# Moving one branch's weight sums out of the marked queue, and one order of four sums

## The chip, the cores and the metric

The kernel runs on one core of one Trainium2 chip. The metric is the device time of one execution in microseconds, as the median of several runs. Engines are named TensorE (PE in the rows; PEld is its weight load), VectorE (DVE), ScalarE (ACT), GpSimd (POOL) and SyncE (SP).

## What is computed

One layer of a streaming encoder on 512 positions of width 1024, all in float32:

```python
h = rmsnorm(x, norm_mix)
u, v, bg, cg, xb, zc, gl = split(h @ w_in)
ya = sgu(gelu(u), gelu(v), ...)          # gated, masked 128x128 blocks
yb = bg * causal_dwconv(cg * xb, conv_b_w)
yc = pool_mixer(zc, pool_w, pool_scale)
g  = sigmoid(gl)                         # three gates, 1024 wide each
merged = g[0] * (ya @ w_br_a) + g[1] * (yb @ w_br_b) + g[2] * (yc @ w_br_c)
x = x + merged @ w_o
h = rmsnorm(x, norm_ffn)
a = causal_dwconv(h @ w_up, ffn_conv_w)
x = x + (silu(a_gate) * a_value) @ w_down
out = rmsnorm(x, norm_f)
```

The change lies around the three branch products (`ya @ w_br_a` and so on) and the three gates' columns of `h @ w_in`.

## The kernel before

**Products in three parts.** A float32 matrix is split into an upper part (ScalarE copies it to the rounded type, `upper`, or negated in `split_negative`, L59 and L63) and a lower part (VectorE subtracts, `lower`, L67 and L64). `mm3` (L81 to L83) issues upper times upper and both mixed products, so each product costs three matmuls of 128 x 512.

**Seven instead of eight.** The branches, the gates and the down projection are 2 x 2 block products done with seven block products (m1 to m7) instead of eight. They need four sums of weight blocks, T1 to T4. For the first two branches VectorE adds the blocks in SBUF (`add_branch`, L166, its adds are L178). For the third branch, the gates and the down projection the sums are made in HBM: a `WeightSums` object (L135) has four HBM tensors; `copy` copies a base block into each and `add` issues accumulating transfers on top. T1 = b11 + b12, T2 = b22 + T1, T3 = b12 + b22, T4 = b21 + T2. So T2's add needs T1, and T4's needs T2. For a gate each block is 1 MB, for a branch 0.5 MB. All these transfers are issued by POOL's queue q0, in the written order (`in_order`, L127). An add waits on POOL until its base copy, and the sum it reads, have landed; what stands behind it on POOL waits too.

**Feeding TensorE.** SP loads blocks of 128 x 1024 weights into raw tiles (`Raws`, L92, queue q1); four may be live, and the next is issued when VectorE has finished with one. `Pieces` (L332) gives the order: branch 0, gate 0, branch 1, gate 1, branch 2, gate 2, one piece for a branch's block product, two for a gate's. Each piece is split into one of four ring slots, which is free again when TensorE has used the piece four before it. A piece is 12 matmuls. The order inside ScalarE's and VectorE's queues is laid out before the run by a planner, which goes by its own estimates of durations; only in the head of the kernel the written order is kept.

**Around the change.** At L634 to L637 POOL, after a tiny wait, issues copies and adds of gate 0's and gate 1's sums. The sums of branch 2 and gate 2 come later, behind marks: the list `behind` (L927 to L930) holds eleven steps (one of four copies, four adds of branch 2; two of two copies, four adds of gate 2), and `next_sum` (L932) takes one off: ScalarE copies a column of the bank o just written to a tiny tile (L936), POOL copies that tile (L407), and so waits until TensorE has come so far; then POOL issues the step. `gate` (L959) calls `next_sum` after each of its seven products, `branch` (L1028) after form s2 for branches 1 and 2. Seven steps therefore fall in gate 0, one in branch 1, three in gate 1.

In `branch` the bank x takes m1, is copied by ScalarE (`copies`, L948, tile bm), and then takes form s2 on top; later x takes s3, VectorE adds it into c (L842), and then a22. So TensorE's s2 waits for bm, and a22 waits for VectorE's c. The tile bm shares its scratch buffers with the gate's last s (L961), which VectorE reads at the end of the gate.

Of the kernel before, what the change touches and what calls it, by code (L numbers as in the profile page):

```python
# [26 lines left out]
def trunk_kernel(  # L27
# [64 lines left out]
    class Raws:  # L92


        def __init__(self):
            self.todo, self.ready, self.live, self.cap = [], [], 0, 4
# [38 lines left out]
    class WeightSums:  # L135
        def __init__(self, name, b11, b12, b21, b22):
            t1, t2, t3, t4 = self.t = [
                dram.tile([P, b11.shape[1], 528], F32, name=f"{name}_t{i + 1}")[:, :, :512] for i in range(4)]
            self.base = [(t1, b11), (t3, b12), (t2, b22), (t4, b21)]
            self.added = [(t1, b12), (t3, b22), (t2, t1), (t4, t2)]  # L140

            self.products = {"m1": b11, "m2": b21, "m3": b22, "m4": t4, "m5": t1, "m6": t2, "m7": t3}

# [96 lines left out]
    def tiny(tag, name):  # L240
        return small.tile([P, 1], F32, tag=tag, name=name)
# [156 lines left out]
    def quarters(half, c0):  # L398
        return [half(k)[:, :, c0 + 512 * h:c0 + 512 * h + 512] for k in range(2) for h in range(2)]

    gate_sums = [WeightSums(f"g{i}", *quarters(lambda k: w_in_v[:, 4 * k:4 * k + 4], 3072 + 1024 * i))
                 for i in range(3)]
    last_branch_sums = WeightSums("br2", *quarters(lambda k: w_br_q[2][k], 0))

    def pool_waits_for(t, name):

        in_order(nc.gpsimd.tensor_copy(tiny(name, name), t[:, 0:1]))  # L407
# [224 lines left out]
        v_gelu(t)  # L632
    v_center()
    pool_waits_for(pw_raw, "begun")  # L634
    for sums in gate_sums[:2]:
        sums.copy()
        sums.add()  # L637

# [181 lines left out]
    def form(tags, name):  # L820

        return [[act.tile([P, 2, 256], F32R, tag=tags[2 * kp + i], name=f"{name}_{p}{kp}")
                 for i, p in enumerate(("hi", "lo"))] for kp in range(2)]
# [17 lines left out]
    def tt(o, a, b, op):  # L841
        nc.vector.tensor_tensor(o, a, b, op=op)  # L842
# [41 lines left out]
    sums = []  # L884
# [39 lines left out]
    nc.vector.tensor_scalar(nrstd1, rstd1, -1.0, None, op0=ALU.mult)  # L924


    behind = [lambda: last_branch_sums.copy()]  # L927
    behind += [lambda: last_branch_sums.add(1)] * 4
    behind += [lambda: gate_sums[2].copy(2)] * 2
    behind += [lambda: gate_sums[2].add(1)] * 4  # L930

    def next_sum(o):  # L932
        if behind:
            n = len(behind)
            mark = tiny(f"mark{n}", f"mark{n}")
            nc.scalar.copy(mark, o[:, 0:1])  # L936
            pool_waits_for(mark, f"passed{n}")
            behind.pop(0)()

    def product(o, st, n, first):  # L940
        for q in range(0, n, 2):
            [w] = pieces.take()
            for k in range(q, q + 2):
                mv = [p[:, 512 * (k - q):512 * (k - q) + 512] for p in w]
                for r in range(2):
                    mm3(o[r], st(k, r), mv, first and k == 0, k == n - 1, more=not first)

    def copies(tag, name, o):  # L948
        got = [scratch(tag, f"{name}{r}") for r in range(2)]
        for r in range(2):  # L950
            nc.scalar.copy(got[r], o[r])
        return got

    def banks(name):
        return [bank(f"{name}{r}") for r in range(2)]
# [72 lines left out]
    def branch(i, form):  # L1028
        c = [[act.tile([P, S], F32, tag=f"m{8 + 2 * t + h}" if i == 0 else f"x{t}{h}", name=f"c{i}{t}{h}")
              for h in range(2)] for t in range(NT)]  # L1030
        x = banks(f"bx{i}")
        product(x, form("a11"), 2, True)
        m1 = copies(0, f"bm1{i}", x)
        d = banks(f"bd{i}")
        product(d, form("s1"), 2, True)
        m5 = copies(1, f"bm5{i}", d)
        product(x, form("s2"), 2, False)
        if i > 0:
            next_sum(x[1])
        m16 = copies(2, f"bm16{i}", x)  # L1040
        a = banks(f"ba{i}")
        product(a, form("a12"), 2, True)
        for r in range(2):
            tt(c[r][0], a[r], m1[r], ALU.subtract)
        product(x, form("s3"), 2, False)
        for r in range(2):
            tt(c[2 + r][1], x[r], m5[r], ALU.add)
        product(d, form("s4"), 2, False)
        for r in range(2):
            tt(c[r][1], d[r], m16[r], ALU.add)  # L1050
        product(x, form("a22"), 2, False)
        for r in range(2):
            nc.scalar.mul(c[2 + r][0], x[r], -1.0)
        return c

    for i in range(3):
        c = branch(i, forms[i])
        if i == 0:
            acc = c
        gate(i, c)  # L1060
# [221 lines left out]
    x = banks("dx")  # L1282
# [83 lines left out]
```

## Time and profile before

| what | value |
|---|---|
| median of 3 runs | 739.06 us (738.57 to 740.81) |
| profiled execution | 736.67 us |
| its span, first to last instruction | 734.9 us |
| TensorE busy | 720.7 us, 98% of the span |
| VectorE, ScalarE, POOL busy | 562.7, 370.6, 62.6 us (77%, 50%, 9%) |
| DMA moved | 150.87 MB, mean 205 GB/s |
| POOL's queue q0, SP's queue q1 | 52.43 MB, 96.76 MB |
| chain that ended last | PE 93%, DVE 3%, DMA 2%, ACT 1% |

The profile is one execution, taken on the core, and its durations belong to that execution alone. The busy time of TensorE is modelled at the ends of matmuls, so the steps between starts say more than the busy share. An idle time in brackets behind a row is that of the engine just before the instruction, with what ended it; a wait for several things is put down to the last of them that the profile can see.

### The profile page before, as it was taken

The numbers are of one execution on the slowest core, as the hardware profiler recorded it, in microseconds if no ns is written. First come the engines' busy times: TensorE is split into PE (matmuls) and PEld (weight loads), VectorE is DVE, ScalarE is ACT, GpSimd is POOL, SyncE is SP. The second block draws the span as 40 slices with busy tenths as digits, with TensorE's granted clock in tenths as the row PEclk, the third lists the DMA queues.
The fourth block names the chain that finished last, engine by engine and source line by source line (L and its number), as shares of the span: only waits on it lengthen the run. The fifth ranks groups of instructions, "written<-read, shape, count | busy, mean of one in ns | idle before, by whom it ended". The sixth has DMA issues, their size and how long they took to land.

```text
span 734.9 us, 8928 instructions
## 1 busy us (share of the span) xinstructions
PE 720.7 (98%) x3258; PEld 594.8 (81%) x3258; DVE 562.7 (77%) x836; ACT 370.6 (50%) x551; POOL 62.6 (9%) x93
## 2 busy tenths in 40 slices
PE   8999999999999998999999999999999999999996
PEld 5888888888877886888888888888888888888885
DVE  6889899889598687677556786766787776997674
ACT  4744144266675565664444443443444444965453
POOL 0041210001221100000012010100000000000110
PEclk9999999999999999999999999999999999999999
DMA  8649999737999996675228999999633232576652
GB/s 254 192 170 283 244 331 237 183 90 232 304 313 313 229 295 199 196 225 183 87 75 264 236 296 285 253 311 220 178 97 105 86 106 82 155 234 201 194 163 114
DMA packets 89211, 150.87 MB, mean 205 GB/s; under 512 B 4008, under 2 KB 39248, under 8 KB 89168
## 3 DMA queue, kind: packets, MB, share of 16 engines
q1 hardware_dynamic: 68607, 96.76, 41.7%
q0 software_dynamic: 19840, 52.43, 29.8%
q10 hardware_dynamic: 720, 1.11, 0.4%
q8 instruction: 25, 0.41, 0.2%
q14 instruction: 19, 0.15, 0.1%
HBM read 148.20 MB, written 54.53 MB: 276 GB/s over the span
## 4 chain that ended last, share of the span: by engine, by line
PE 93%; DVE 3%; DMA 2%; ACT 1%; issue 1%; SPq 0%; ACTq 0%
PE pug L83 5%; PE puv L83 5%; PE pug L81 5%; PE puv L81 5%; PE puv L82 5%; PE pug L82 5%; PE gx L82 3%; PE gx L81 3%; PE gx L83 3%; PE dx L83 2%; PE dx L82 2%; PE po L81 2%; PE dx L81 2%; PE po L83 2%; PE po L82 2%; PE gd L83 1%
## 5 line engine op out<-in xcount | busy, mean ns | idle before, releaser
L81 PE MATMUL pug<-h2T_hi,ring_hi 128*128 128x512 f32 x176 | 68.7, 390 | 0.0
L83 PE MATMUL pug<-h2T_hi,ring_lo 128*128 128x512 f32 x176 | 68.5, 389 | 0.0
L82 PE MATMUL puv<-h2T_lo,ring_hi 128*128 128x512 f32 x176 | 68.5, 389 | 0.0
L81 PE MATMUL puv<-h2T_hi,ring_hi 128*128 128x512 f32 x176 | 68.5, 389 | 0.0
L82 PE MATMUL pug<-h2T_lo,ring_hi 128*128 128x512 f32 x176 | 68.5, 389 | 0.0
L83 PE MATMUL puv<-h2T_hi,ring_lo 128*128 128x512 f32 x176 | 68.5, 389 | 0.0
L67 DVE TENSOR_TENSOR ring_lo<-raw_g_m,ring_hi 128x1024 fp32r<-128x1024 f32 x30 | 36.6, 1224 | 29.2 <-ACT ring_hi L59 29.1
L59 ACT CAST ring_hi<-raw_ug 128x1024 fp32r<-128x1024 f32 x22 | 23.3, 1057 | 47.4 <-PE pug L82 42.2
L67 DVE TENSOR_TENSOR ring_lo<-raw_uv,ring_hi 128x1024 fp32r<-128x1024 f32 x22 | 26.9, 1222 | 25.1 <-ACT ring_hi L59 25.1
L59 ACT CAST ring_hi<-raw_g_m 128x1024 fp32r<-128x1024 f32 x30 | 31.5, 1055 | 26.2 <-DMA raw_g_m<-in_w_in_dram 9.6
L67 DVE TENSOR_TENSOR ring_lo<-raw_d_m,ring_hi 128x1024 fp32r<-128x1024 f32 (+1 forms) x30 | 35.8, 1204 | 9.0 <-ACT ring_hi L59 8.9
L59 ACT CAST ring_hi<-raw_d_m 128x1024 fp32r<-128x1024 f32 (+1 forms) x30 | 29.5, 982 | 18.6 <-PE da L83 8.2
L82 PEld LDWEIGHTS puv<-h2T_lo,ring_hi 128*128 128x128 f32 x176 | 33.0, 188 | 6.9
L82 PEld LDWEIGHTS pug<-h2T_lo,ring_hi 128*128 128x128 f32 x176 | 33.0, 188 | 6.9
L83 PEld LDWEIGHTS pug<-h2T_hi,ring_lo 128*128 128x128 f32 x176 | 33.0, 188 | 6.9
L83 PEld LDWEIGHTS puv<-h2T_hi,ring_lo 128*128 128x128 f32 x176 | 33.0, 188 | 6.9
L81 PEld LDWEIGHTS puv<-h2T_hi,ring_hi 128*128 128x128 f32 x176 | 33.0, 188 | 6.9
L81 PEld LDWEIGHTS pug<-h2T_hi,ring_hi 128*128 128x128 f32 x176 | 33.0, 188 | 6.8
L67 DVE TENSOR_TENSOR ring_lo<-raw_ug,ring_hi 128x1024 fp32r<-128x1024 f32 x22 | 26.9, 1222 | 8.8 <-ACT ring_hi L59 8.7
L59 ACT CAST ring_hi<-raw_uv 128x1024 fp32r<-128x1024 f32 x22 | 23.2, 1056 | 19.1 <-PE puv L82 18.8
L1136 ACT ACTIVATE av<-av_y,colv 128x512 f32<-128x512 f32 x22 | 16.0, 727 | 27.9 <-DVE av_y L1134 26.9
L1136 ACT ACTIVATE ag<-ag_y,colv 128x512 f32<-128x512 f32 x22 | 15.8, 720 | 21.5 <-DVE ag_y L1134 21.5
(432 smaller groups left out, 2028.9 us busy)
## 6 DMA issues: line engine op xcount, KB each, us to landing
g_t<-in_w_in_dram POOLq DMA_DIRECT2D x18, 1024.0 KB, 13.2
d_t<-in_w_down_dram POOLq DMA_DIRECT2D x6, 2816.0 KB, 27.2
raw_g_m<-g_t SPq DMA_DIRECT2D x24, 512.0 KB, 4.2
raw_ug<-in_w_up_dram SPq DMA_DIRECT2D x22, 512.0 KB, 6.2
raw_uv<-in_w_up_dram SPq DMA_DIRECT2D x22, 512.0 KB, 5.1
raw_d_m<-d_t SPq DMA_DIRECT2D x20, 512.0 KB, 3.9
raw_g_m<-in_w_in_dram SPq DMA_DIRECT2D x18, 512.0 KB, 10.0
raw_d_m<-in_w_down_dram SPq DMA_DIRECT2D x15, 512.0 KB, 3.3
```

Of the source, the lines that this page charges most:

```text
L59: return keep(nc.scalar.copy(hi, src))
L67: return keep(nc.vector.tensor_tensor(lo, src, hi.bitcast(F32), op=ALU.subtract))
L81: keep(nc.tensor.matmul(o, st[0], mv[0], start=first, stop=False, **skip))
L82: keep(nc.tensor.matmul(o, st[0], mv[1], start=False, stop=False, **skip))
L83: keep(nc.tensor.matmul(o, st[1], mv[0], start=False, stop=last, **skip))
L1136: nc.scalar.activation(a, y, AF.Copy, scale=ffn_w(2, c))
```

## The change

Three edits. The order of base copies and adds in every `WeightSums` is T1, T2, T3, T4 instead of T1, T3, T2, T4 (it holds for all gates, branch 2 and the down projection). Branch 2's four copies and four adds are issued right behind gate 1's, without marks. Of the list behind marks eight steps remain, gate 2's copies and adds one by one; `branch` no longer takes a step. So gate 0's seven products take seven steps and gate 1's first product the eighth.

```diff
         def __init__(self, name, b11, b12, b21, b22):
             t1, t2, t3, t4 = self.t = [
                 dram.tile([P, b11.shape[1], 528], F32, name=f"{name}_t{i + 1}")[:, :, :512] for i in range(4)]
-            self.base = [(t1, b11), (t3, b12), (t2, b22), (t4, b21)]
-            self.added = [(t1, b12), (t3, b22), (t2, t1), (t4, t2)]
+            self.base = [(t1, b11), (t2, b22), (t3, b12), (t4, b21)]
+            self.added = [(t1, b12), (t2, t1), (t3, b22), (t4, t2)]
...
     pool_waits_for(pw_raw, "begun")
-    for sums in gate_sums[:2]:
+    for sums in gate_sums[:2] + [last_branch_sums]:
         sums.copy()
         sums.add()
...
-    behind = [lambda: last_branch_sums.copy()]
-    behind += [lambda: last_branch_sums.add(1)] * 4
-    behind += [lambda: gate_sums[2].copy(2)] * 2
+    behind = [lambda: gate_sums[2].copy(1)] * 4
     behind += [lambda: gate_sums[2].add(1)] * 4
...
         product(x, form("s2"), 2, False)
-        if i > 0:
-            next_sum(x[1])
         m16 = copies(2, f"bm16{i}", x)
```

## Rows read from the trace of the kernel before

**Rows 1.** TensorE's timeline: start us, duration, line, tiles, [idle before <-releaser]

```profile
216.93 0.50 PE L81 MATMUL bx<-ring_hi,f_hi 128*128 128x512 f32 x1 [0.54 <-ACT bm L951]
...
227.03 0.39 PE L83 MATMUL bd<-ring_hi,f_lo 128*128 128x512 f32 x1
...
229.14 0.47 PE L81 MATMUL bx<-ring_hi,fo_hi 128*128 128x512 f32 x1 [1.72 <-DVE c L842]
...
275.27 0.39 PE L83 MATMUL bd<-ring_hi,f_lo 128*128 128x512 f32 x1
...
278.37 0.65 PE L81 MATMUL bx<-ring_hi,f_hi 128*128 128x512 f32 x1 [2.71 <-ACT bm L951]
...
282.35 0.40 PE L82 MATMUL bx<-ring_lo,f_hi 128*128 128x512 f32 x1
```

**Rows 2.** Window: span, busy of PE, PEld, DVE, ACT, POOL; PEclk; DMA share; GB/s

```profile
278.40:281.80 3.40, 3.40 (x8) 2.64 (x9) 3.10 (x3) 2.44 (x4) 0.00 (x0) 0.52 0.59 166
```

**Rows 3.** Timeline of ScalarE, columns as in the first group

```profile
163.74 1.06 ACT L63 ACTIVATE ring_hi<-raw_g_m 128x1024 fp32r<-128x1024 f32 x1 [1.17 <-PE ba L83]
...
226.07 1.06 ACT L63 ACTIVATE ring_hi<-raw_g_m 128x1024 fp32r<-128x1024 f32 x1 [3.62 <-DMA raw_g_m<-in_w_in_dram]
...
270.04 1.05 ACT L59 CAST ring_hi<-raw_br_m 128x1024 fp32r<-128x1024 f32 x1 [4.37 <-PE gx L82]
...
277.74 1.19 ACT L951 COPY bm<-bx 128x512 f32<-128x512 f32 x2 [1.41 <-DVE c L842]
```

**Rows 4.** Timeline of VectorE

```profile
228.31 1.28 DVE L842 TENSOR_TENSOR c<-bx,bm 128x512 f32<-128x512 f32 x2
...
271.13 1.23 DVE L67 TENSOR_TENSOR ring_lo<-raw_br_m,ring_hi 128x1024 fp32r<-128x1024 f32 x1 [1.31 <-ACT ring_hi L59]
```

**Rows 5.** Timeline of POOL: the sums' transfers

```profile
132.77 1.02 POOL L151 DMA_DIRECT2D g_t<-g_t  x1 [12.56 <-issue]
...
177.89 2.81 POOL L146 DMA_DIRECT2D br_t<-in_w_br_c_dram  x4
...
206.83 1.55 POOL L146 DMA_DIRECT2D g_t<-in_w_in_dram  x2
...
259.36 1.02 POOL L151 DMA_DIRECT2D g_t<-g_t  x1 [10.31 <-issue]
```

**Rows 6.** Timeline of SP: the loads, merged

```profile
155.77 8.45 SPq L106 DMA_DIRECT2D raw_g_m<-in_w_in_dram  x4
...
218.53 5.57 SPq L106 DMA_DIRECT2D raw_g_m<-in_w_in_dram  x4
...
261.47 1.84 SPq L106 DMA_DIRECT2D raw_br_m<-br_t  x2
```

**Rows 7.** Three more windows, columns as in the second group

```profile
100.00:204.50 104.50, 104.50 (x463) 86.53 (x462) 88.09 (x126) 52.15 (x74) 12.54 (x16) 1.00 0.82 225
...
145.00:155.00 10.00, 10.00 (x46) 8.29 (x45) 9.15 (x12) 3.77 (x6) 0.00 (x0) 1.00 0.00 0
...
211.00:221.00 10.00, 9.46 (x41) 7.16 (x40) 10.00 (x12) 8.91 (x18) 1.77 (x3) 1.00 1.01 362
```

**Rows 8.** Tile view of one load each, issued at 163.9, 245.5 and 265.1

```profile
DMA to landing us min/median/max: 3.5/3.5/3.5
...
DMA to landing us min/median/max: 13.6/13.6/13.6
...
DMA to landing us min/median/max: 7.4/7.4/7.4
```

**Rows 9.** DMA queues: packets, MB, share; 211 to 221, then 247 to 256

```profile
q0 software_dynamic: 932, 3.60, 100.8%
...
q0 software_dynamic: 592, 1.18, 70.5%
...
q1 hardware_dynamic: 594, 1.15, 38.8%
```

**Rows 10.** Page, DMA issues: count, KB each, median us to landing

```profile
g_t<-in_w_in_dram POOLq DMA_DIRECT2D x18, 1024.0 KB, 13.2
```

## The prediction

> **What bounds the kernel now.** TensorE does, nearly everywhere. So I read first the timeline of TensorE's matmuls and looked only for places where the step from one start to the next is longer than usual: what TensorE doesn't lose, no other engine can give back. In [rows 1] the usual step follows from the starts at 216.93 and 227.03 us, 44 steps apart: 10.10 / 44 = 0.23 us. Between 20 us and the tail I find three places with more than 0.2 us to lose, all in the second and third branch:
>
> - A1, at 216.93: TensorE idle 0.54 us ahead of bx (branch 1, form s2), released by ScalarE's copy bm. Loss 0.5 us.
> - A2, at 229.14: 2.11 us after the last matmul of bd, less a step of 0.23: loss 1.9 us. Released by VectorE (L842, c).
> - B, at 278.37: from 275.27 to 282.35 us lie 11 steps, 7.08 - 11 * 0.23 = 4.6 us lost. The wait itself (on ScalarE's bm in branch 2) is 2.71 us; the rest is the granted clock, 0.52 in the 3.4 us behind the gap [rows 2], the lower of its two levels, after TensorE had stood still.
>
> Together 7.0 us, 0.95% of the run. That is all there is to win; the head, the tail and the dense rest aren't touched by the edit.
>
> Next I asked who was late at each of them, in the timelines of ScalarE and VectorE. At A2, ScalarE stood 3.62 us until 226.07 for the first weights of gate 1 [rows 3]; VectorE's lower half of that split came behind it, and only then c<-bx,bm at 228.31, which frees the bank that TensorE wants [rows 4]. So one late transfer in VectorE's fixed order holds TensorE. SP issued it at 218.53 [rows 6]: 7.5 us to landing, where a like transfer with nothing beside it took 3.5 [rows 8]. In those microseconds POOL's copies for gate 2 (two issued from 206.83, two behind the next mark) [rows 5] were running: from 211 to 221 us POOL's queue q0 had the DMA engines whole, 3.60 MB in 10 us [rows 9].
>
> At B, ScalarE stood 4.37 us and began a raw_br_m at 270.04 [rows 3]. The row names a matmul, but the raw was issued at 261.47 [rows 6], and SP's next but one, issued at 265.10, took 7.4 us [rows 8], to 272.5; I read 270.0 as the landing, 8.5 us after the issue. Beside it ran the last add of gate 2, issued at 259.36 [rows 5]. VectorE waited 1.31 us for that split at 271.13 [rows 4], and from there its timeline shows no idle time up to the c that ScalarE's bm waited for until 277.74 [rows 3]. So A2 and B start as transfers that met POOL's sums. A1 doesn't: VectorE is busy 10.00 of the 10 us around it [rows 7], with four extra adds (L178) per branch.
>
> **The change, part by part.**
>
> *Branch 2's sums without marks.* Four copies and four adds of 0.5 MB leave their five places among the marks and stand behind gate 1's last add, issued at 132.77 [rows 5]. POOL, SP's loads and the DMA engines are what they pass: from 145 to 155 us the DMA share is 0.00 [rows 7], and the first loads of gate 0 come at 155.77 [rows 6]. With marks its issues took from 177.89 until gate 2's copies at 206.83, 29 us, and a landing more. Eight issues with three dependent landings I estimate at 25 to 40 us, so they end between 160 and 175 us. ScalarE's split of gate 0's first weights starts only at 163.74, when TensorE frees a slot [rows 3]; the load issued at 155.77 may take 8.0 us instead of 3.5 before that moves. I book 0; bounds 0 and +5 us (latency of 13.6 as in [rows 8]: 5.6 us late, in the pattern of A2).
>
> *Three marks gone* (11 become 8; branch 1 has none any more): each a tiny ScalarE copy, a tiny POOL copy and waits, all beside matmuls. 0 us on the path; bounds -0.2 and 0 at A1, where one stood in ScalarE's queue.
>
> *Gate 2's sums from the first mark on.* The marks come every (206.83 - 177.89) / 5 = 5.8 us [rows 5]. So four copies of 1 MB go at about 178, 183, 189 and 195 us, one each, where before 2 MB of branch 2's copies went at once and 2 MB of its adds followed. The first add goes at 201; a landing takes POOL some 13 us [rows 10], so the second and third are held in POOL's queue and issued at 212 to 215; the fourth at gate 1's first mark, near 237. What is queued behind POOL's wait is only the next mark's copy and sums: nobody on the path before gate 2 reads T2. Over gate 0 some 5 MB move instead of 4 plus the 4 MB burst at its end. Booked 0 for gate 0: from 100 to 204.5 us, gate 1's sums and then branch 2's beside it, TensorE was busy all 104.50 us [rows 7]. Bounds 0 and +3 us (one block of loads late: 12 matmuls of 0.23 us).
>
> *A2.* Its load at 218.53 now meets two adds instead of the end of a burst of copies. An add shares: from 247 to 256 us q0 moved 1.18 MB and SP's q1 1.15 MB [rows 9], so 0.52 MB take 9 * 0.52 / 1.15 = 4.1 us. Ahead of it lie the 3.5 us of an undisturbed load less its 0.52 MB at 362 GB/s [rows 7], 1.4 us: 2.1. So I estimate the landing at 218.5 + 6.2 = 224.7, 1.3 us sooner. Loss left 1.9 - 1.3 = 0.6 us; bounds 0 (adds late) and 2.9 (B's load, first in its queue beside a fresh add, took 8.5 us: landing 227.0). I take the share, since here the adds have been running for some us when the load comes.
>
> The Trainium skill (DMA: Bandwidth & Descriptors, section Queues, rings and completion order) states that each DMA engine goes round-robin between the queue rows that it has work for, a packet at a time. The adds agree (1.18 to 1.15 MB [rows 9]); the copies from 218.5 to 221 don't, q0 kept everything. By the rule alone A2 would already have had its half and would not improve: 1.3 us less gain.
>
> *B.* No sum runs after about 250 us; the load takes 3.5 instead of 8.5 us, and the split is bound by its ring slot, about 265, not 270. VectorE then gets 5 us for five splits and adds that it now does in a row; the wait was 2.71. Loss left 0 us; bounds 0 and 3.3 (VectorE's own 1.31 us of idle is all that comes back).
>
> *T2 ahead of T3* in copies and adds: T2's add waits for T1's landing, so T3's stands behind it on POOL; T4's wait then overlaps T3's transfer. Each gate has one empty latency either way. 0 us; what it serves, gate 2's T2 first, isn't waited for.
>
> Sum: A1 stays 0.5, A2 leaves 0.6, B 0: 7.0 - 1.1 = 5.9 us less. The profiled execution took 736.67 us with a span of 734.9; the three timed runs have the median 739.06 (738.57 to 740.81). I take the difference off the median: 733.2 us. 0.3% (2.2 us) is about what a measurement of this kernel can tell from no change.
>
> **The rivals.**
>
> *VectorE, not the load, sets B.* Its queue is gapless from 271.13 to B's end, which speaks for it; against it, 4 us of ScalarE's idle ahead say the work could have been done earlier. Then only 1.3 us come back at B and the low clock stays, and nothing sure at A2: 739.06 - 1.3 = 737.8, no change that can be told.
>
> *Gate 1's first loads still late.* The adds held on POOL come out at 212 to 215, straight onto the load of 218.53. Against: adds share, the copies didn't [rows 9]. A2 stays at 1.9: 739.06 - 4.6 = 734.5.
>
> *Slower: the chain of branch 2's sums ends too late.* Place: POOL, 133 to 178 us [rows 5]. If its last add lands after the first mark (177.9), gate 2's sums all slip and reach B again, so the 7.0 us stay, while gate 0's loads from 155.77 on meet adds that they didn't meet. With a landing later than 163.7 VectorE stands in branch 0 as it did at A2, and TensorE loses about what B lost: 739.06 + 4.6 = 743.7. It decides at a chain of 45 us instead of my 25 to 40. The planner that lays out each engine's order beforehand may place a split badly with the same result; nothing in the trace tells.
>
> **How the numbers follow.** Forecast (731.5 to 735.5) 0.47; late loads in gate 1 (734.5) 0.20; VectorE at B (737.8) 0.17; slower (743.7) 0.16. Faster by over 0.3%, below 736.8: 0.47 + 0.20 + 0.03 of the VectorE case = 0.70. Within: 0.14. Slower: 0.16. The range runs from 731.2 (all 7.0 us gone and 0.9 of spread between runs) to 741.2, which leaves out most of the slower case; the likeliest case's own range is 731.5 to 735.5.
>
> **What would show it.** Right: the DMA share from 145 to 155 us far from 0; br_t's last add issued before 170; no add issued after 250; bx of branch 2 follows bd within 0.5 us at full clock; the wait at bx of branch 1 (form a22) below 1 us. Wrong in part: bx still waits on bm although its load landed 3.5 us after the issue (VectorE). Wrong altogether: TensorE's first gap in branch 0 or gate 0, between 150 and 210 us, or a gap after 284.

## The result, and the profile after

The changed kernel takes 731.12 us (median of 4, 730.71 to 733.10) against 738.82 (median of 4, 737.35 to 740.81) for the kernel before: ratio 0.9899, 95% interval 0.9870 to 0.9929, so 5.2 to 9.6 us less. The profiled executions have spans of 734.9 and 729.3 us.

TensorE's list of waits after the change (us in total, times, longest) has one entry left behind the head of the kernel:

```profile
PE bx L81 <- DVE c L842: 1.6, 1, 1.6
```

The gaps of [rows 1], in TensorE's timeline after the change:

```profile
215.36 0.39 PE L83 MATMUL bd<-ring_hi,f_lo 128*128 128x512 f32 x1
215.59 0.39 PE L81 MATMUL bx<-ring_hi,f_hi 128*128 128x512 f32 x1
...
274.35 0.39 PE L83 MATMUL bd<-ring_hi,f_lo 128*128 128x512 f32 x1
274.57 0.39 PE L81 MATMUL bx<-ring_hi,f_hi 128*128 128x512 f32 x1
```

A1 and B are gone: form s2 follows bd one step (0.23 us) later in branch 1 (215.59) and in branch 2 (274.57). A2 is still there: a wait of 1.6 us on the same c. The sums, in POOL's timeline after:

```profile
125.03 1.02 POOL L151 DMA_DIRECT2D g_t<-g_t  x1 [6.70 <-issue]
125.66 3.21 POOL L146 DMA_DIRECT2D br_t<-in_w_br_c_dram  x4
...
155.54 0.89 POOL L151 DMA_DIRECT2D br_t<-br_t  x1 [4.36 <-issue]
178.26 0.77 POOL L146 DMA_DIRECT2D g_t<-in_w_in_dram  x1
...
199.93 1.19 POOL L151 DMA_DIRECT2D g_t<-in_w_in_dram  x1
211.44 1.06 POOL L151 DMA_DIRECT2D g_t<-g_t  x1 [5.11 <-DMA g_t<-in_w_in_dram]
213.29 1.15 POOL L151 DMA_DIRECT2D g_t<-in_w_in_dram  x1
239.17 1.02 POOL L151 DMA_DIRECT2D g_t<-g_t  x1
```

Branch 2's sums stand between 125.66 and 155.54, gate 2's last add at 239.17 instead of 259.36 [rows 5]. Windows after (span, busy of PE, PEld, DVE, ACT, POOL, granted clock, DMA share, GB/s), for the three of [rows 7]:

```profile
100.00:204.50 104.50, 104.50 (x463) 86.60 (x462) 87.32 (x124) 53.34 (x75) 15.22 (x21) 1.00 0.94 265
145.00:155.00 10.00, 10.00 (x46) 8.29 (x45) 9.15 (x13) 3.66 (x5) 1.98 (x2) 1.00 0.74 119
211.00:221.00 10.00, 10.00 (x45) 8.28 (x45) 9.62 (x13) 9.40 (x16) 3.00 (x3) 1.00 0.84 145
```

The stretch from 145 to 155 us, empty before, now carries 0.74 of the DMA engines' time, and TensorE stays busy throughout. Nor were gate 0's first loads hurt: ScalarE still waits there for TensorE's slot, as at 163.74 in [rows 3].

```profile
164.11 1.06 ACT L63 ACTIVATE ring_hi<-raw_g_m 128x1024 fp32r<-128x1024 f32 x1 [1.17 <-PE ba L83]
```

### The profile page after: what moved, and what is told of

Same layout as the page of the kernel before. It is cut to its first block, busy times and chain, and to the rows that moved or that the text cites. A ratio compares the mean times of both kernels' runs of the same rounds, so it can differ in the third digit from the quotient of the medians.

```text
span 729.3 us, 8922 instructions
## 1 busy us (share of the span) xinstructions
PE 718.5 (99%) x3258; PEld 594.4 (82%) x3258; DVE 562.7 (77%) x836; ACT 370.2 (51%) x548; POOL 60.2 (8%) x90
## 4 chain that ended last, share of the span: by engine, by line
PE 94%; DMA 3%; ACT 1%; DVE 1%; issue 0%; SPq 0%; ACTq 0%
PE pug L83 5%; PE puv L83 5%; PE pug L81 5%; PE puv L82 5%; PE pug L82 5%; PE puv L81 5%; PE gx L83 3%; PE gx L81 3%; PE gx L82 3%; PE dx L82 2%; PE dx L83 2%; PE po L81 2%; PE dx L81 2%; PE po L83 2%; PE po L82 2%; PE dd L82 1%
## 5 line engine op out<-in xcount | busy, mean ns | idle before, releaser
L1132 ACT ACTIVATE av<-av_y,colv 128x512 f32<-128x512 f32 x22 | 15.9, 724 | 27.9 <-DVE av_y L1130 26.9
```

What stands on the lines that cost most here:

```text
L1132: nc.scalar.activation(a, y, AF.Copy, scale=ffn_w(2, c))
```

## The experiments

Each run is compared with runs of the kernel before on the same chip. The ratio in brackets has its 95% interval behind it.

### One edit alone: the order

```diff
# kernel before
-            self.base = [(t1, b11), (t3, b12), (t2, b22), (t4, b21)]
-            self.added = [(t1, b12), (t3, b22), (t2, t1), (t4, t2)]
+            self.base = [(t1, b11), (t2, b22), (t3, b12), (t4, b21)]
+            self.added = [(t1, b12), (t2, t1), (t3, b22), (t4, t2)]
```

> The kernel before with the order T1, T2, T3, T4 alone; marks and places as before. Theory (the gain comes from where the sums stand in time, not from their order): the gaps in branch 1 (0.5 and 1.9 us) and in branch 2 (4.6 us) stay within 1 us each; 738.8 us, within 2. Rival (the order itself gives the gain, T3 no longer beside T1): the gap in branch 2 falls below 1 us and the time by 4 us or more, below 735.

Measured 739.38 us (1.0013, 0.9994 to 1.0033): no change. But the gaps moved more than the theory allowed. TensorE's waits of over 1 us from branch 1 to branch 2, in its timeline:

```profile
228.85 0.47 PE L81 MATMUL bx<-ring_hi,fo_hi 128*128 128x512 f32 x1 [2.43 <-DVE c L842]
...
...
268.43 0.47 PE L81 MATMUL gx<-ring_hi,hT_hi 128*128 128x512 f32 x1 [2.02 <-DVE m L842]
283.48 0.50 PE L81 MATMUL bx<-ring_hi,f_hi 128*128 128x512 f32 x1 [2.27 <-ACT bm L951]
```

The wait at A1 is gone, B is smaller, and gate 1 itself waits now. The order alone shifts where the loads come late; the median shows no gain from it.

### One edit alone: branch 2's sums unmarked

```diff
# kernel before
-    for sums in gate_sums[:2]:
+    for sums in gate_sums[:2] + [last_branch_sums]:
...
-    behind = [lambda: last_branch_sums.copy()]
-    behind += [lambda: last_branch_sums.add(1)] * 4
+    behind = [lambda: None] * 5
```

> The kernel before with branch 2's sums unmarked, the old order, and gate 2's sums at their old marks (five empty marks keep the places). Theory (the gap in branch 2 is gate 2's last add beside the loads; the first gap in branch 1 is the backlog of gate 0's late loads): the last add is still issued near 258, the gap in branch 2 stays at 3 to 5 us, the second gap in branch 1 (1.9) stays within 1 us, the first (at form s2) goes: 1 us less, 737.5 to 738.5. Rival 1 (VectorE's adds make the first gap): it stays too, nothing changes, 738.8. Rival 2 (moving branch 2's sums is the whole gain): 732 to 733.

Measured 735.86 us (0.9956, 0.9934 to 0.9979): 1.5 to 4.9 us less, where 1 us was expected. Branch 2's last sum has moved by 168.4 us, and no other moves until gate 2's first copy is issued at 207.08. TensorE runs through A1 (no wait there), and B is as large as ever, a wait of 3.18 us with the low clock (0.50) behind it. (The profiled execution, 738.67 us, took longest of the twelve, so B may be smaller in the others.) TensorE's timeline and a window:

```profile
216.17 0.39 PE L83 MATMUL bd<-ring_hi,f_lo 128*128 128x512 f32 x1
216.40 0.39 PE L81 MATMUL bx<-ring_hi,f_hi 128*128 128x512 f32 x1
...
280.35 0.50 PE L81 MATMUL bx<-ring_hi,f_hi 128*128 128x512 f32 x1 [3.18 <-ACT bm L950]
```

```profile
281.90:284.50 2.60, 2.60 (x8) 2.02 (x7) 1.88 (x2) 1.50 (x2) 0.00 (x0) 0.50 0.66 201
```

So A1 goes when no sum runs beside gate 0's loads, though VectorE's adds are all still there; and the move of branch 2's sums is not the whole gain.

### The last add put back to its old time

```diff
# changed kernel
     behind = [lambda: gate_sums[2].copy(1)] * 4
-    behind += [lambda: gate_sums[2].add(1)] * 4
+    behind += [lambda: gate_sums[2].add(1)] * 3
+    behind += [lambda: None] * 4
+    behind += [lambda: gate_sums[2].add(1)]
...
-            mark = tiny(f"mark{n}", f"mark{n}")
+            mark = tiny(f"mark{n % 8}", f"mark{n}")
```

The twelve marks share eight tiny tiles.

> The changed kernel, but gate 2's last add waits for four further marks, so that it is issued near 257 to 260 us as before the change; all else as changed. Theory (that one add beside branch 2's loads is the gap in branch 2): the gap comes back with 2 to 4.6 us, low clock included; 733 to 736. Rival (the backlog of gate 1's late loads made it, and those are gone): no gap above 0.5 us in branch 2, 731.1 within 0.7.

Measured 731.62 us (0.9909, 0.9880 to 0.9937), and no gap in branch 2: the theory falls. The timelines of POOL and SP show why:

```profile
259.86 1.02 POOL L151 DMA_DIRECT2D g_t<-g_t  x1 [0.31 <-issue]
```

```profile
256.58 2.73 SPq L106 DMA_DIRECT2D raw_br_m<-br_t  x2
```

The add is issued within 0.5 us of its old time, but branch 2's second load is issued at 256.58, ahead of it; in the kernel before that load went at 261.47 [rows 6]. Gate 1's loads were not late, so these weren't either.

### T3's add held back

```diff
# changed kernel
-    behind += [lambda: gate_sums[2].add(1)] * 4
+    behind += [lambda: gate_sums[2].add(1)] * 2
+    behind += [lambda: None]
+    behind += [lambda: gate_sums[2].add(1)] * 2
```

> The changed kernel with one empty mark between the adds of T2 and T3 of gate 2, so that T3's add and T4's are issued in gate 1 (near 237 and 242) and only T2's add is under way when gate 1's first load is issued. Theory (the gap left in branch 1 is the time that POOL's queue still has adds after 216): q0 is empty near 221, the load lands near 222 to 223 instead of 225.1, and the gap falls from 1.9 us to 0 to 0.5; the two adds then run from 239 to 257 beside gate 1's loads and cost 0 to 2 us there; 729.5 to 731.5. Rival (the load's own first microseconds are slow beside any add): the gap in branch 1 stays above 1.5 us; 731 to 733.

Measured 731.35 us (0.9911, 0.9876 to 0.9946). A2 is gone, and in its place B is back in part. POOL's and TensorE's timelines (this is TensorE's only wait in branches 1 and 2):

```profile
236.69 1.16 POOL L151 DMA_DIRECT2D g_t<-in_w_in_dram  x1
241.77 1.02 POOL L151 DMA_DIRECT2D g_t<-g_t  x1 [0.31 <-issue]
```

```profile
275.16 0.50 PE L81 MATMUL bx<-ring_hi,f_hi 128*128 128x512 f32 x1 [1.50 <-ACT bm L951]
```

Two adds beside gate 1's loads, near 237 and 242, make a wait of 1.5 us in branch 2 some 30 us later, though no sum is issued after 241.77 and the last has moved by 257.2. So B is, for one part, the backlog of gate 1. The rival's premise holds all the same: beside T2's add the load's first data came 3.4 us after its issue (217.03), but the add ended soon enough for the gap to go.

### The kernel before with its last add alone moved

```diff
# kernel before
-    behind += [lambda: gate_sums[2].add(1)] * 4
+    behind += [lambda: gate_sums[2].add(1)] * 3
+    behind += [lambda: None] * 4
+    behind += [lambda: gate_sums[2].add(1)]
...
-            mark = tiny(f"mark{n}", f"mark{n}")
+            mark = tiny(f"mark{n % 8}", f"mark{n}")
```

> The kernel before with gate 2's last add alone moved, from 259 us to gate 1's last product (issued near 270); the adds beside gate 1's loads (near 240 and 244) stay. Theory, formed anew (the gap in branch 2 has two parts: gate 1's loads late behind those two adds push branch 2's loads back, and the last add then meets them): branch 2's second load lands about 5 us sooner than 270, the gap falls from 4.6 to between 1.2 and 2.5 us and the low clock goes; the gaps in branch 1 stay; 2 to 3.5 us less than before, ratio 0.995 to 0.998. Rival 1 (the last add alone is the gap): it falls below 0.5 us, ratio near 0.994. Rival 2 (the backlog alone): it stays above 3.5 us, ratio near 1.

Measured 736.24 us (0.9975, 0.9957 to 0.9993). The add was issued later than meant, at 283.63, which is behind bx of branch 2 (281.44) all the same. TensorE's timeline, and the window behind the gap:

```profile
217.27 0.50 PE L81 MATMUL bx<-ring_hi,f_hi 128*128 128x512 f32 x1 [0.54 <-ACT bm L953]
...
231.22 0.47 PE L81 MATMUL bx<-ring_hi,fo_hi 128*128 128x512 f32 x1 [3.44 <-DVE c L842]
...
281.44 0.50 PE L81 MATMUL bx<-ring_hi,f_hi 128*128 128x512 f32 x1 [1.84 <-ACT bm L953]
```

```profile
281.50:284.90 3.40, 3.40 (x15) 2.80 (x16) 3.10 (x3) 3.30 (x6) 3.14 (x2) 1.00 0.59 164
```

B's wait falls from 2.71 to 1.84 us and the granted clock behind it is 1.00 instead of 0.52 [rows 2]. The loss falls from 4.6 us to about 2.0 (the wait and its edges). A1's wait is unchanged; A2's, expected to stay, is twice that of [rows 1], with a granted clock of 0.50 behind it (232.8 to 235.5 us). So B had two parts: some 2 us of backlog from gate 1, and some 2.5 us from the last add meeting the belated loads, most of that the low clock. These are readings of one execution each; those of the other runs agree (see B below).

### Three adds left out

```diff
# changed kernel
-    behind += [lambda: gate_sums[2].add(1)] * 4
+    behind += [lambda: gate_sums[2].add(1)]
+    behind += [lambda: None] * 3
```

> The changed kernel without the adds of gate 2's T2, T3 and T4 (left out: these three sums are not formed; marks and all other work as they were). It shows what gate 2's sums still cost. Theory: from 212 us on no sum moves, gate 1's first load lands in 3.5 us, the last gap in branch 1 (1.9 us) goes and nothing else changes: span 727.3, 729.0 to 729.7 us. Rival (VectorE's own work at the turn of branch 1 holds TensorE): the gap stays above 1 us.

Measured 729.01 us (0.9878, 0.9846 to 0.9911), span 727.2. TensorE has no wait left between 100 and 340 us (window, columns as above):

```profile
100.00:340.00 240.00, 240.00 (x1076) 198.81 (x1075) 194.82 (x256) 137.77 (x189) 18.10 (x24) 1.00 0.79 228
```

So A2, too, is the sums, and 729.0 is what is left when they cost nothing.

### Copies in pairs

```diff
# changed kernel
-    behind = [lambda: gate_sums[2].copy(1)] * 4
+    behind = [lambda: gate_sums[2].copy(2)] * 2
     behind += [lambda: gate_sums[2].add(1)] * 4
```

> The changed kernel with gate 2's four copies in pairs at the first two marks, so that all its adds lie in gate 0: the first add near 189, all done near 223. Theory (gate 0 has loads to spare for 5 MB of sums, but 7 MB before 211 us use it up): the gap left in branch 1 falls below 1 us, and in its place the second half of gate 0 or branch 1's first pieces wait 1 to 5 us; 730 to 735. Rival (gate 0 has spare time for all of it): no gap before branch 1, 729.0 to 730.0.

Measured 735.90 us (0.9960, 0.9941 to 0.9979): 4.8 us more than the changed kernel, and just above the range of the theory. Gate 0's end and branch 1 wait, as A1 did:

```profile
205.58 0.47 PE L81 MATMUL gx<-ring_hi,hT_hi 128*128 128x512 f32 x1 [0.61 <-DVE m L842]
...
219.04 0.49 PE L81 MATMUL bx<-ring_hi,f_hi 128*128 128x512 f32 x1 [1.63 <-ACT bm L949]
```

The DMA queues from 177 to 206 us (packets, MB, share of 16 engines) say what a load costs here. First this kernel, then the changed one:

```profile
q0 software_dynamic: 1616, 5.24, 58.2%
q1 hardware_dynamic: 2156, 4.17, 42.1%
```

```profile
q0 software_dynamic: 1342, 4.71, 49.1%
q1 hardware_dynamic: 2668, 5.14, 49.0%
```

With 0.53 MB more of sums, SP's loads got 0.97 MB less, nearly two blocks. One copy at each mark is near what gate 0 bears. A2's gap is gone here.

### The old order within the changed kernel

```diff
# changed kernel
-            self.base = [(t1, b11), (t2, b22), (t3, b12), (t4, b21)]
-            self.added = [(t1, b12), (t2, t1), (t3, b22), (t4, t2)]
+            self.base = [(t1, b11), (t3, b12), (t2, b22), (t4, b21)]
+            self.added = [(t1, b12), (t3, b22), (t2, t1), (t4, t2)]
```

> The changed kernel with the old order T1, T3, T2, T4. T3's add no longer waits on POOL for T1's landing: it is issued near 206 instead of 213, T2's near 212. Theory (the gap left in branch 1 is set by how long adds run after 216): q0 is done near 223 instead of 229, gate 1's first load lands 1 to 2 us sooner and the 1.9 us gap falls to 0 to 1; 729.5 to 730.5. Rival (the load's start is held by whatever add is under way at 216): the gap stays at 1.9 and the time at 731.1.

Measured 729.28 us (0.9871, 0.9847 to 0.9894). POOL's timeline, the place of ScalarE's wait, and TensorE's A2:

```profile
199.70 1.19 POOL L151 DMA_DIRECT2D g_t<-in_w_in_dram  x1
206.05 1.17 POOL L151 DMA_DIRECT2D g_t<-in_w_in_dram  x1
212.38 1.04 POOL L151 DMA_DIRECT2D g_t<-g_t  x1 [1.00 <-DMA g_t<-in_w_in_dram]
```

```profile
223.35 1.06 ACT L63 ACTIVATE ring_hi<-raw_g_m 128x1024 fp32r<-128x1024 f32 x1 [3.11 <-DMA raw_g_m<-in_w_in_dram]
```

```profile
226.01 0.39 PE L83 MATMUL bd<-ring_hi,f_lo 128*128 128x512 f32 x1
226.41 0.47 PE L81 MATMUL bx<-ring_hi,fo_hi 128*128 128x512 f32 x1
```

T3's add goes at 206.05 instead of 213.29, and gate 1's first load has landed by 223.35 instead of 225.18. A2 shrinks from 2.0 us between starts to 0.40. The load, issued at 216.01, does not start sooner: its first data come at 219.4, 3.4 us later, as in the changed kernel (216.24 and 219.7). What ends sooner is the sharing. The DMA queues from 221 to 226 us, to be compared with those of the changed kernel under A2 below:

```profile
q1 hardware_dynamic: 926, 1.77, 92.5%
q0 software_dynamic: 24, 0.04, 4.0%
```

The changed kernel and the old order again, on one chip, beside each other:

> The changed kernel again, beside the next run on the same chip: 7 to 8 us less than before, with the one gap of 1.8 us in branch 1 left.

> The changed kernel with the old order T1, T3, T2, T4 again, on the same chip as the run above. Theory (T3's add needs no other sum and so fills the time in which T2's waits for T1): 1.5 to 2 us less than the changed kernel, gap in branch 1 below 0.5 us. Rival (chance in the place of one landing): within 0.7 us of the changed kernel.

Measured: the changed kernel 731.25 us (0.9902, 0.9879 to 0.9926; 729.95 to 731.36), with the old order 729.68 (0.9882, 0.9857 to 0.9908; 728.84 to 729.90). A2's wait is 1.91 us in the one and 0.34 in the other. The old order with the other two edits beats both kernels, by 1.6 us the changed one, and stands within 0.7 us of the run without the three adds.

## Why the prediction was right, and where not

**The sum.** Predicted 5.9 us less (733.2 from 739.06); the profiled spans differ by 5.6 and the medians by 7.7, more than the 7.0 that I called all there is to win. TensorE's gaps account for the spans. Set side by side matmul by matmul, the execution of the changed kernel loses 0.4 us in the head, gains 1.0 at A1 (the wait, and late starts beside it), 0.2 to 0.3 around A2 and 4.6 at B, and nothing after. So the sum is near by luck in part: some 1.1 us too much at A2 and 1.0 too little at A1 cancel. The medians say more because the profiled execution of the kernel before, 736.67 us, lies 2.2 us below its kernel's median, while that of the changed kernel, 731.16, lies at its median. Where the other executions lose these 2.2 us is not shown. The kernel before varies more: in the profile of the run with its last add moved, code up to branch 1 being that of before, A2's wait is 3.44 us where [rows 1] have 1.72. The execution of [rows 1] may have caught a mild A2.

Of the signs that I named for being right, the full stretch from 145 to 155 us, the last issues of branch 2's and gate 2's sums, and branch 2 without a gap all came. The wait below 1 us at A2 did not.

**Branch 2's sums: right.** They run in the empty stretch, the last is issued at 155.54 and has moved by 163.2 (I had them ending between 160 and 175), and the load at 156.13 costs nothing at the ring slot (164.11). The slower rival's point of decision, the first mark at 178.26, was never near. They had 7 us more than I reckoned with: gate 1's last add is issued at 125.03, not at 132.77 [rows 5].

**Gate 2's marks: right.** Forecast 178, 183, 189, 195, 201, 212 to 215, near 237; the trace has 178.26 to 199.93, 211.44, 213.29 and 239.17. Gate 0 took it without a gap. Copies in pairs show how close that was.

**A1: the reading was wrong.** I put it down to VectorE, busy 10.00 of 10 us [rows 7], and kept the 0.5. VectorE is nearly as busy after (9.62 of 10), and the gap is gone; it went without sums in gate 0, and grew (1.63 us of wait) with more of them. VectorE had been worked into a backlog by gate 0's late loads. ScalarE's waits for gate 0's weights, from 176 to 216 us, come to 6.2 us before, to none after, to 11.1 with copies in pairs. With the order alone they come to 3.3, and A1 is absent though sums run, which points to how late the loads are and not to the sums as such. SP's timelines show the lateness one step earlier: branch 1's loads, each issued when VectorE has freed a tile, were issued from 195.87 us before, from 193.69 after.

```profile
195.87 8.36 SPq L106 DMA_DIRECT2D raw_br_b<-in_w_br_b_dram  x4
```

```profile
193.69 8.56 SPq L106 DMA_DIRECT2D raw_br_b<-in_w_br_b_dram  x4
```

**A2: mis-sized.** The term was the landing of the load, 2.1 us ahead of its data and 4.1 us of shared transfer. The issue is at 216.24, ScalarE begins at 225.18, 8.9 us later instead of 6.2:

```profile
225.18 1.06 ACT L63 ACTIVATE ring_hi<-raw_g_m 128x1024 fp32r<-128x1024 f32 x1 [4.78 <-DMA raw_g_m<-in_w_in_dram]
```

The DMA queues of the changed kernel, from 215 to 219 us and then from 221 to 226:

```profile
q0 software_dynamic: 404, 0.82, 112.5%
```

```profile
q0 software_dynamic: 330, 0.67, 72.4%
q1 hardware_dynamic: 324, 0.63, 38.2%
```

The share was right (0.63 MB in 5 us, so 0.52 MB in 4.1). The start was not: until 219 the load has no row at all. From 219 to 220 us it has six packets; with three adds left out the same load, issued at 215.94, has its first by 217:

```profile
q1 hardware_dynamic: 6, 0.01, 3.7%
...
q1 hardware_dynamic: 5, 0.01, 7.8%
```

So its first data came 3.5 us after the issue (219.7) beside a running add, and 1.0 us after it (216.97) with none: 2.5 of the 2.7 us that I was short. The price that I set aside, B's load with 8.5 us, was the right one. It is the sharing behind the start that the old order removes (above), so neither part alone is A2. So the second rival, gate 1's first loads still late, held for A2, while A1 gave what A2 didn't.

The Trainium skill's rule of round-robin between queue rows (DMA: Bandwidth & Descriptors, section Queues, rings and completion order) agrees with the trace once both queues have data (0.67 to 0.63 MB). It doesn't tell of the microseconds before, in which q0 had everything, and these made most of the difference.

**B: the gain right, the cause half right.** I named the last add. Put back alone, it costs nothing; taken away alone, it leaves some 2.0 us. The other half is the backlog that the adds near 240 and 244 make among gate 1's loads, which is also what brought branch 2's loads late enough to meet the last add. SP's rows for branch 2's second and third load show it in the other runs (unmarked only; last add moved; T3 held; the changed kernel):

```profile
262.80 2.52 SPq L106 DMA_DIRECT2D raw_br_m<-br_t  x2
...
265.91 1.88 SPq L106 DMA_DIRECT2D raw_br_m<-br_t  x2
...
259.65 1.85 SPq L106 DMA_DIRECT2D raw_br_m<-br_t  x2
...
257.47 1.68 SPq L106 DMA_DIRECT2D raw_br_m<-br_t  x2
```

I take the time from the end of such a row to the moment at which bx could follow bd. It is 12.2 us in the kernel before [rows 6], 11.7 unmarked, 11.7 with the last add moved, 12.0 with T3 held and 12.8 with the order alone: all five have a gap. It is 15.4 us in the changed kernel and 15.9 with the last add put back: neither has one, though in the latter the add is issued 15.4 us ahead of that moment. Among the five the gap is 4.6 to 4.7 us where the last add is issued some 15 to 16 us ahead of that moment (before, unmarked), and 1.7 to 2.4 where it is issued long before or after it. The rival that VectorE sets B is answered by the same runs: its queue is full only because the splits come late.

**T2 ahead of T3: booked at 0, costs 1.6 us.** I saw that T3's add stands behind T2's wait on POOL and said that T4's wait makes up for it. It doesn't where the end of the chain meets other loads: for 11 us after T1's add POOL issues no other (199.93 to 211.44), and T3's transfer falls on gate 1's first load. Where a list runs without marks and meets nothing, the new order ends sooner: gate 1's last add is issued at 125.03 and branch 2's at 155.54, with the old order (rest as changed) at 133.82 and 160.53. I had both orders equal there.

## What to carry to other kernels

A gap of the busiest engine that names a compute engine may still be a transfer's: follow the loads some tens of microseconds back, through the queue that fell behind. Background transfers belong where the foreground's queue is empty, and spread out, one at a time. In a list of dependent transfers whose end meets loads, try putting one that waits for nothing behind each one that others wait for; in this kernel that was worth 1.6 us at gate 2.

## What the runs showed of the hardware

A load newly issued on SP's queue can wait for its first data while POOL's queue moves sums: 3.1 us beside copies (kernel before, issued 218.53, first data at 221.6) and 3.5 us beside an add (changed kernel, issued 216.24, first data at 219.7). With nothing beside it that wait was 1.0 us (three adds left out, issued 215.94), and a whole 0.52 MB load took 3.5 us [rows 8]. It is not so for every load: in the changed kernel one issued at 182.81 beside a copy had its first data at 183.6.

The low clock took some 1.7 us of B's price of 4.6: behind the wait of 2.71 us eight steps of TensorE, from 278.37 us on, take 0.43 us each instead of 0.23. The wait of 1.84 us at the same place left the granted clock at 1.00. The length of one wait doesn't decide it: behind waits of 2.43 and 2.27 us (order alone) the granted clock was 1.00, behind 2.02 us (order alone, a wait of 0.76 us ahead of it) 0.57, and behind 1.63 us (copies in pairs, shorter waits ahead of it) 0.53.
